# Second parts of 28 weight units kept in DRAM between two token groups of a diffusion layer kernel

## The chip, the cores and the metric

One core of one Trainium2 chip. The metric is the device time of one launch in microseconds. Three runs were made before the change; the figure is their median, and one more execution was profiled.

## The reference

A layer is run for 128 context tokens and for 1024 latent tokens with the same weights. What matters here, per group of tokens (shapes are tokens by features, D = 1024):

```python
h = rmsnorm(x, norm1_g) * (1.0 + scale1) + shift1
z = h @ w_in                      # zu, zv, zq, zf_fw, zf_bw, zi, zg, za, zb
y_a = chunk_gmlp(zu, zv, ...)     # gated mixing inside chunks of 128 tokens
y_b, s_fin = hgrn2_bidir(zq, zf_fw, zf_bw, zi, zg, ...)      # two scans over all tokens
mix = (sigmoid(za) * (y_a @ w_proj_a) + sigmoid(zb) * (y_b @ w_proj_b)) @ w_out
x = x + gate1 * mix
h = rmsnorm(x, norm2_g) * (1.0 + scale2) + shift2
q = (h @ w_q).reshape(n_tok, 8, 2, 128)
s = einsum('thpc,hpkc->thpk', q, sub_keys)    # 16 score rows of 128 keys for each token
# top 16 of each row, best 16 of the sums of two rows, softmax: 128 experts for each token
x = x + gate2 * sum_e gelu(h . u_tab[e]) * g_e * v_tab[e]
```

All inputs and outputs are float32.

## The kernel before

The tokens are nine tiles of 128: tile 0 is the context, tiles 5 to 8 are group GA, tiles 1 to 4 group GB. The kernel goes through these stages: modulation vectors (`ada`), the context's scan and its group, the scans of all eight latent tiles (4 heads), `group(GA)`, `group(GB)`, and the dense expert stage.

The weights come in units of 128 x 1024 values, stacked in `wst` in the order of their use. `unit(u)` (line 181) loads a unit through SP's DMA queue into one of three buffers `wraw`. A float32 product is made of three fast ones (`mmx`, line 124): each operand is a rounded part H and the rest L, and H times H, L times H and H times L are added up. So for the latent tokens `unit` makes two tiles of each unit with `split` (line 98): ScalarE copies the raw values into `wH` with rounding, and VectorE subtracts `wH` from the raw values into `wL`. `wH` and `wL` have two buffers each. The context's group uses the raw values as they are (`native`).

One call of `group` (line 571) runs over these units, counted from `U_GR` = 16: 0 to 3 and 4 to 7 give rows of zg and zv for the four tiles of the group (`proj_rows`, 24 matmuls of 512 columns for a unit), 8 to 11 give zu, then 24 units give za, zb and the two mixing projections in turn, 8 give w_out, and 44 to 59 are the sixteen query units. For each query unit TensorE makes the queries (`pq`) and then the scores against 128 keys for each of the four tiles (`psc`), and VectorE takes the top 16 of each tile with `top16` (line 414): five passes over 128 values with three loads of match values.

Work of a group that was done before fills in. `combine` (choosing the best 16 of 256 sums, on VectorE) and `build_G` (matrices of gate values for the dense experts, on TensorE, ScalarE and VectorE) wait in lists, and `tick()` at each unit puts a few steps of them into the program. Tokens of tiles 0 to 3 take their experts by `gather` (line 801): for each of 256 rows POOL issues an indirect load of one expert row for each of 128 tokens into one of four buffers, and VectorE multiplies it (`jk`, line 814) or adds it up (`acc`, line 829). Such VectorE instructions are `paced`: a scheduler may not put them ahead of the instruction that is `anchors[0]`, the subtraction of some units ago.

The instructions of each engine are put in order by a scheduler that works by its own costs; on the chip each engine and each DMA queue runs its list in order. POOL's queue takes the gathers, the few small POOL instructions, two loads of 2 MB (`hTBr`) and two of 2.5 MB (`h2DH`, `h2DL`, line 990) from DRAM. All else is on SP's queue.

Of the kernel before, what the change touches and what calls it, by code (L numbers as in the profile page):

```python
# [9 lines left out]
F32 = mybir.dt.float32  # L10
# [5 lines left out]
AF = mybir.ActivationFunctionType  # L16
# [23 lines left out]
GI = 4  # L40

U_ZI, U_HG, U_GR = 0, 4, 16
GATHER = [0, 1, 2, 3]
DENSE = [5, 6, 7, 8, 4]
ND = len(DENSE)
# [6 lines left out]
def hybrid_kernel(ctx, tc, x_all, pos, c2t, w_ada, b_ada, wst, wspt, bsp, lbraw, vecs, fng, skt, state,  # L52
                  ut, urow, vrow, masks, ident_d, small, y_p, y_s, ns):
    nc = tc.nc
    V, A, P, G = nc.vector, nc.scalar, nc.tensor, nc.gpsimd

    consts = ctx.enter_context(tc.tile_pool(name="consts", bufs=1, side="left", reuse_waits="tile"))
    dram = ctx.enter_context(tc.tile_pool(name="dram", bufs=1, space=bass.MemoryType.DRAM))
# [14 lines left out]
    o_d = dram.tile([NT, 128, 512], F32, name="o_d")  # L73
    tvi_d = dram.tile([NT, 128, 512], F32, name="tvi_d")
    h2r_d = dram.tile([NT, 128, D], F32, name="h2r_d")


    ident = consts.tile([128, 128], F32, name="ident")
# [18 lines left out]

    def split(src, H, L):
        A.activation(H, src, AF.Copy)  # L99
        return V.tensor_tensor(out=L, in0=src, in1=H.bitcast(F32), op=OP.subtract)  # L100

    anchors = deque()

    def anchor(ins, keep):

        anchors.append(ins)
        while len(anchors) > keep:
            anchors.popleft()
# [34 lines left out]
    wp = ph1.enter_context(tc.tile_pool(name="wp", bufs=2, side="right", reuse_waits="tile"))  # L143

    nload = [0]

    def load_unit(src, native=True):

# [32 lines left out]
    def unit(u, native=False, src=None):  # L181
        tick()
        raw = load_unit(wst[u] if src is None else src, native)
        if native:
            return [raw]
        H = wp.tile([128, 1024], F32R, name="wH", bufs=2)
        L = wp.tile([128, 1024], F32R, name="wL", bufs=2)
        anchor(split(raw, H, L), 2)
        return [H, L]


# [220 lines left out]
    GA, GB = [5, 6, 7, 8], [1, 2, 3, 4]  # L412

    def top16(gp, s, v_, i_, n, V=V):
        V.max(v_[:, 0:8], s)
        V.max_index(i_[:, 0:8], v_[:, 0:8], s)
        m = s if gp is None else gp.tile([128, 128], F32, name="mrep", bufs=2)
        V.match_replace(m[:, :n], v_[:, 0:8], s, -3.0e38)
        V.max(v_[:, 8:16], m[:, :n])
        V.max_index(i_[:, 8:16], v_[:, 8:16], m[:, :n])  # L420

    def combine(gp, t, tv, ti, al=None, c4=None, V=V, h0=0, h1=8, res=None):

# [147 lines left out]
    def group(gp, tiles, hpar, native):  # L571
        n = len(tiles)
# [37 lines left out]
        u = U_GR  # L610
# [126 lines left out]
        tv = [gp.tile([128, 8, 2, 16], F32, name="tv", bufs=n) for _ in range(n)]  # L737
# [6 lines left out]
        for b in range(16):  # L744
            if b == 8:
                for i in split_at:
                    res = gp.tile([128, 384], F32, name="res", bufs=1).rearrange("p (a b) -> p a b", a=3)
                    halves[i] = res
                    choose_q.append(combine(gp, tiles[i], tv[i], ti[i], h1=4, res=res))
                    rate["choose"] = 1.5  # L750
            w = unit(u + 44 + b, native)
            skb = gp.tile([128, 128], F32, name="skb", bufs=2)
            nc.sync.dma_start(skb, skt[:, b, :])
            ps = pmm("pq")
            projT(ps[:, :T], w, opd_q)
            qs = h512("qs")
            A.activation(qs[:, :T], ps[:, :T], AF.Copy)
            pss = ptp("psc")
            for i in range(n):
                P.matmul(pss[:, i * 128:(i + 1) * 128], qs[:, i * 128:(i + 1) * 128], skb, start=True, stop=True)  # L760
            for i in range(n):
                top16(gp, pss[:, i * 128:(i + 1) * 128], tv[i][:, b // 2, b % 2, :], ti[i][:, b // 2, b % 2, :], 128)
        rate["gather"] = before
        for i in range(n):
            t = tiles[i]
# [217 lines left out]
    for z in range(2):  # L983
        G.dma_start(hTBr[z], hT_d[z])
    rate.update(gather=RATE[2], choose=RATE[3], build=RATE[5])
    group(gp, GB, hTBr, False)
    rate.update(choose=0, gather=0, build=0)
    h2D = bigpair("h2D", TD)
# [214 lines left out]
```

## Time and profile before

| | |
|---|---|
| runs | 3636.42, 3621.89, 3634.37 us; median 3634.37 us |
| the profiled execution | 3629.96 us |
| its span, first to last instruction | 3628.2 us |
| TensorE matmuls busy | 3336.8 us (92% of the span) |
| VectorE busy | 2817.6 us (78%) |
| ScalarE, POOL busy | 1121.3 us (31%), 1429.2 us (39%) |
| moved from and to DRAM | 971.12 MB, mean 268 GB/s |

Read the busy shares as means over stages: the dense stage, from 1727 us to the end, is more than half of the span. PE in the tables is TensorE's matmul, PEld its weight load, DVE is VectorE, ACT ScalarE, SP the engine whose queue issues most transfers. The matmuls of one stage overlap in the profile, so the distance from one start to the next tells more than one duration.

### The profile page before, as it was taken

How to read it: one execution, taken by the hardware profiler on the slowest of the kernel's cores; microseconds unless marked ns; L12 is line 12 of the kernel's file. 1: busy time of each engine (PE TensorE's matmuls, PEld its weight loads, DVE VectorE, ACT ScalarE, POOL GpSimd, SP SyncE). 2: the span in 40 equal slices, each digit the busy share in tenths (PEclk: the TensorE clock that was granted, in tenths of full speed). 3: DMA queues.
4: the chain of work that ended last, by engine and by line, in shares of the span. 5: the costliest groups of instructions: out<-in, count | busy, mean ns of one | idle time of the engine just before them, and what ended most of it. 6: DMA issues, size and time to landing. Idle time of an engine off the chain costs nothing. (4 is left out here: it accounts for less than half of the span.)

```text
span 3628.2 us, 48825 instructions
## 1 busy us (share of the span) xinstructions
PE 3336.8 (92%) x17547; PEld 2764.3 (76%) x17547; DVE 2817.6 (78%) x5427; ACT 1121.3 (31%) x2095; POOL 1429.2 (39%) x1128
## 2 busy tenths in 40 slices
PE   8898999899887999877889999989999999999997
PEld 4386888775665676666788898889898888898996
DVE  2317678785899888697888888888887888788887
ACT  2512443321323655625322222222222222222222
POOL 0102102553112322200365664655555456555653
PEclk9899999999999999999999999999999999999998
DMA  7787324789534778643898997998998799988986
GB/s 282 287 294 274 113 72 132 257 313 342 168 127 141 271 255 325 248 144 117 291 332 299 326 327 268 336 326 306 324 319 320 245 343 333 324 305 316 337 320 247
DMA packets 361957, 971.12 MB, mean 268 GB/s; under 512 B 32721, under 2 KB 142673, under 8 KB 356081
## 3 DMA queue, kind: packets, MB, share of 16 engines
q0 software_dynamic: 149824, 546.37, 42.4%
q1 hardware_dynamic: 211888, 421.62, 33.6%
q8 instruction: 138, 2.26, 0.3%
q14 instruction: 107, 0.87, 0.1%
HBM read 897.07 MB, written 70.80 MB: 267 GB/s over the span
## 5 line engine op out<-in xcount | busy, mean ns | idle before, releaser
L811 POOL DMA_INDIRECT gu<-in_urow_dram,ix x512 | 688.2, 1344 | 1004.7 <-DVE jk L814 421.9
L824 POOL DMA_INDIRECT gv<-in_vrow_dram,ix x512 | 687.3, 1342 | 819.5 <-DVE acc L829 412.2
L814 DVE SCALAR_TENSOR_TENSOR jk<-gu,h2r 128x1024 f16<-128x1024 f32 x512 | 625.2, 1221 | 127.9 <-DMA gu<-in_urow_dram,ix 121.8
L829 DVE SCALAR_TENSOR_TENSOR acc<-gv,act,acc 128x1024 f32<-128x1024 f32 x508 | 651.3, 1282 | 45.2 <-DMA gv<-in_vrow_dram,ix 37.5
L129 PE MATMUL pH<-h2DH,uH 128*128 128x320 f32 x2016 | 626.5, 311 | 10.6 <-DVE accd L1061 8.2
L131 PE MATMUL pH<-h2DH,uL 128*128 128x320 f32 x2016 | 623.7, 309 | 1.1 <-DVE uL L100 1.1
L130 PE MATMUL pH<-h2DL,uH 128*128 128x320 f32 x2016 | 624.2, 310 | 0.0
L129 PEld LDWEIGHTS pH<-h2DH,uH 128*128 128x128 f32 x2016 | 380.4, 189 | 21.7 <-DVE accd L1061 13.4
L130 PEld LDWEIGHTS pH<-h2DL,uH 128*128 128x128 f32 x2016 | 380.4, 189 | 4.5
L131 PEld LDWEIGHTS pH<-h2DH,uL 128*128 128x128 f32 x2016 | 380.2, 189 | 1.7 <-DVE uL L100 1.7
L129 PE MATMUL pout<-vH,aH 128*128 128x512 f32 x768 | 300.6, 394 | 21.9 <-ACT vH L99 16.1
L99 ACT ACTIVATE vH<-vr 128x1024 fp32r<-128x1024 f32 x128 | 133.2, 1058 | 564.0 <-DMA vr<-in_vrow_dram 295.8
L131 PE MATMUL pout<-vH,aL 128*128 128x512 f32 x768 | 301.7, 393 | 4.1 <-DVE aL L100 4.1
L130 PE MATMUL pout<-vL,aH 128*128 128x512 f32 x768 | 301.7, 393 | 1.1 <-DVE vL L100 1.1
L129 PE MATMUL prot<-vH,aH 128*128 128x512 f32 x512 | 209.2, 409 | 54.4 <-DVE accd L1061 50.1
L99 ACT ACTIVATE wH<-wraw 128x1024 fp32r<-128x1024 f32 x118 | 124.9, 1058 | 401.9 <-PE pq L130 163.7
L100 DVE TENSOR_TENSOR vL<-vr,vH 128x1024 fp32r<-128x1024 f32 x128 | 156.1, 1220 | 91.0 <-ACT vH L99 90.9
L560 PE MATMUL pG<-oh 128*128 128x128 f16 x1280 | 176.8, 316 | 33.3 <-ACT Gs L563 21.6
L560 PEld LDWEIGHTS <-oh 128*128 128x128 f16 x1280 | 147.2, 131 | 78.0 <-issue 63.2
L130 PE MATMUL prot<-vL,aH 128*128 128x512 f32 x512 | 206.2, 403 | 0.0
L131 PE MATMUL prot<-vH,aL 128*128 128x512 f32 x512 | 205.5, 401 | 0.0
L99 ACT ACTIVATE aH<-a 128x640 fp32r<-128x640 f32 x128 | 94.2, 737 | 358.3 <-DVE a L1078 352.2
(345 smaller groups left out, 6306.4 us busy)
## 6 DMA issues: line engine op xcount, KB each, us to landing
wraw<-in_wst_dram SPq DMA_DIRECT2D x216, 512.0 KB, 4.6
vr<-in_vrow_dram SPq DMA_DIRECT2D x128, 512.0 KB, 6.8
ur<-in_ut_dram SPq DMA_DIRECT2D x126, 512.0 KB, 6.6
G_d<-Gs SPq DMA_DIRECT2D x40, 1024.0 KB, 5.0
Gt<-G_d SPq DMA_DIRECT2D x160, 256.0 KB, 9.6
wraw<-in_w_ada_dram SPq DMA_DIRECT2D x48, 512.0 KB, 5.5
gu<-in_urow_dram,ix POOLq DMA_INDIRECT x512, 6.7
gv<-in_vrow_dram,ix POOLq DMA_INDIRECT x512, 6.9
```

Source lines behind the costliest of these rows:

```text
L99: A.activation(H, src, AF.Copy)
L100: return V.tensor_tensor(out=L, in0=src, in1=H.bitcast(F32), op=OP.subtract)
L129: P.matmul(ps, a[0], b[0], start=first, stop=False)
L130: P.matmul(ps, a[0], b[1], start=False, stop=False)
L131: P.matmul(ps, a[1], b[0], start=False, stop=last)
L560: P.matmul(pg[:, :, tt], oh[:, 0, :, tt], og[a][:, :, tt], start=(a == 0), stop=(a == 1))
L811: G.indirect_dma_start(out=ur, out_offset=None, in_=urow, in_offset=bass.IndirectOffsetOnAxis(ap=ix[:, c:c + 1], axis=0))
L814: paced(V.scalar_tensor_tensor(jk, ur, 1.0, h2r, op0=OP.mult, op1=OP.mult, accum_out=dots[:, k:k + 1]))
L824: G.indirect_dma_start(out=vr, out_offset=None, in_=vrow, in_offset=bass.IndirectOffsetOnAxis(ap=ix[:, c:c + 1], axis=0))
L829: paced(V.scalar_tensor_tensor(acc, vr, act[:, k:k + 1], acc, op0=OP.mult, op1=OP.add))
```

## The change

For 28 of the 60 units of a group, 0 to 11 and 44 to 59 (`KEPT`), the first latent group GA writes `wL` to DRAM on SP's queue after the subtraction. The second group GB loads and rounds the raw unit as before, but takes `wL` from DRAM by a load on POOL's queue in place of the subtraction. For these units there is no anchor in GB any more; in the queries the last instruction of the first tile's `top16` becomes one.

```diff
+KEPT = set(range(0, 12)) | set(range(44, 60))
...
+    wL_d = dram.tile([60, 128, 1024], F32, name="wL_d")
...
+    second = [False]
...
         H = wp.tile([128, 1024], F32R, name="wH", bufs=2)
         L = wp.tile([128, 1024], F32R, name="wL", bufs=2)
+        if src is None and u - U_GR in KEPT and second[0]:
+            A.activation(H, raw, AF.Copy)
+            G.dma_start(L, wL_d[u - U_GR])
+            return [H, L]
         anchor(split(raw, H, L), 2)
+        if src is None and u - U_GR in KEPT:
+            nc.sync.dma_start(wL_d[u - U_GR], L.bitcast(F32))
         return [H, L]
...
-        V.max_index(i_[:, 8:16], v_[:, 8:16], m[:, :n])
+        return V.max_index(i_[:, 8:16], v_[:, 8:16], m[:, :n])
...
             for i in range(n):
-                top16(gp, pss[:, i * 128:(i + 1) * 128], tv[i][:, b // 2, b % 2, :], ti[i][:, b // 2, b % 2, :], 128)
+                ins = top16(gp, pss[:, i * 128:(i + 1) * 128], tv[i][:, b // 2, b % 2, :], ti[i][:, b // 2, b % 2, :], 128)
+                if i == 0 and tiles is GB:
+                    anchor(ins, 2)
...
     rate.update(gather=RATE[2], choose=RATE[3], build=RATE[5])
+    second[0] = True
     group(gp, GB, hTBr, False)
```

The scheduler orders the program anew. Line numbers in the changed program are a few higher: 193 is the new load of L, 197 its store, 157 the load of the raw weights, 762 that of the keys (`skb`), 822 and 835 the gathers, 1002 the loads for the dense stage.

POOL at the start of GB, before. The rows are gathers of expert rows (`gu`, `gv`) and the small instructions of a norm:

```order
L824 DMA gv<-in_vrow_dram,ix_2105 128x1024 x9
L811 DMA gu<-in_urow_dram,ix_2105 128x1024 x5
L94 TENSOR_SCALAR rstd<-ss 128x1
L95 TENSOR_TENSOR rstd<-rstd,nhalf 128x1
L94 TENSOR_SCALAR rstd<-ss 128x1
```

The same place with the change:

```order
L835 DMA gv<-in_vrow_dram,ix_2106 128x1024 x9
L822 DMA gu<-in_urow_dram,ix_2106 128x1024
L193 DMA wL<-wL_d 128x1024
L822 DMA gu<-in_urow_dram,ix_2106 128x1024
L193 DMA wL<-wL_d 128x1024
L822 DMA gu<-in_urow_dram,ix_2106 128x1024
L193 DMA wL<-wL_d 128x1024 x2
L822 DMA gu<-in_urow_dram,ix_2106 128x1024
L193 DMA wL<-wL_d 128x1024
L822 DMA gu<-in_urow_dram,ix_2106 128x1024
L193 DMA wL<-wL_d 128x1024 x4
L822 DMA gu<-in_urow_dram,ix_2106 128x1024 x3
```

The loads for the first nine units of GB stand between the gathers, four of them in a row; three more follow among the norm's instructions.

SP at the first queries of GA, before. `h2T_d` takes the normed tokens for the dense stage, `wraw` is a unit's load:

```order
L734 DMA h2T_d<-h2L 128x4x128 x2
L753 DMA skb<-in_skt_dram 128x128
L154 DMA wraw<-in_wst_dram 128x1024
L753 DMA skb<-in_skt_dram 128x128 x2
L154 DMA wraw<-in_wst_dram 128x1024 x2
```

With the change:

```order
L743 DMA h2T_d<-h2L 128x4x128 x2
L197 DMA wL_d<-wL 128x1024
L762 DMA skb<-in_skt_dram 128x128 x2
L157 DMA wraw<-in_wst_dram 128x1024
L762 DMA skb<-in_skt_dram 128x128
L197 DMA wL_d<-wL 128x1024
L157 DMA wraw<-in_wst_dram 128x1024
L197 DMA wL_d<-wL 128x1024
L157 DMA wraw<-in_wst_dram 128x1024
```

A store of L now stands ahead of each load of raw weights.

POOL at the queries of GB, before:

```order
L95 TENSOR_TENSOR rstd<-rstd,nhalf 128x1 x2
L990 DMA h2DH<-h2T_d 128x5120
L990 DMA h2DL<-h2T_d 128x5120
L824 DMA gv<-in_vrow_dram,ix_2105 128x1024 x3
L94 TENSOR_SCALAR rstd<-ss 128x1
```

With the change:

```order
L193 DMA wL<-wL_d 128x1024 x2
L1002 DMA h2DH<-h2T_d 128x5120
L193 DMA wL<-wL_d 128x1024
L835 DMA gv<-in_vrow_dram,ix_2106 128x1024
L193 DMA wL<-wL_d 128x1024
L835 DMA gv<-in_vrow_dram,ix_2106 128x1024
L1002 DMA h2DL<-h2T_d 128x5120
L193 DMA wL<-wL_d 128x1024 x2
L835 DMA gv<-in_vrow_dram,ix_2106 128x1024 x2
L193 DMA wL<-wL_d 128x1024
L835 DMA gv<-in_vrow_dram,ix_2106 128x1024
L193 DMA wL<-wL_d 128x1024 x7
```

The loads of L for the third query on stand around the two loads for the dense stage and around the last gathers of the first gathered tile.

## Rows read from the trace of the kernel before

**Rows 1.** The page's first line.

```profile
span 3628.2 us, 48825 instructions
```

**Rows 2.** Busy time by stretch of the span; the columns stand in the first row.

```profile
core 0: us, PE busy (x) PEld busy (x) DVE busy (x) ACT busy (x) POOL busy (x), PEclk, DMA share, GB/s
600.00:700.00 100.00, 86.16 (x437) 70.44 (x436) 77.92 (x125) 36.97 (x70) 48.11 (x38) 0.91 0.64 210
925.00:1036.00 111.00, 107.32 (x516) 85.91 (x515) 102.22 (x493) 30.24 (x42) 13.34 (x10) 0.98 0.51 162
1036.00:1138.00 102.00, 83.37 (x355) 65.20 (x354) 97.60 (x408) 36.70 (x53) 14.47 (x16) 0.92 0.34 108
1138.00:1200.00 62.00, 51.46 (x224) 36.33 (x223) 57.99 (x177) 24.57 (x56) 15.02 (x12) 0.94 0.47 161
1200.00:1500.00 300.00, 274.24 (x1418) 193.30 (x1417) 255.79 (x442) 169.25 (x498) 101.85 (x81) 0.97 0.80 293
1530.00:1653.00 123.00, 101.63 (x473) 80.98 (x472) 111.84 (x574) 27.85 (x37) 6.73 (x7) 0.92 0.42 146
1727.00:3628.00 1901.00, 1799.25 (x9888) 1624.31 (x9888) 1588.90 (x2146) 471.77 (x689) 1056.10 (x784) 0.97 0.89 312
```

**Rows 3.** TensorE's waits from 1036 to 1140 us: total us, times, longest.

```profile
PE prow L130 <- DVE wL L100: 9.9, 2, 5.9
PE pzu L131 <- DVE wL L100: 6.3, 1, 6.3
```

**Rows 4.** TensorE's groups, 1524 to 1665 us: count | busy, mean ns | idle before.

```profile
L131 PE MATMUL pq<-h2H,wL 128*128 128x512 f32 x123 | 50.6, 415 | 16.8 <-DVE wL L100 16.8
```

**Rows 5.** VectorE's groups, 1036 to 1140 us.

```profile
L100 DVE TENSOR_TENSOR wL<-wraw,wH 128x1024 fp32r<-128x1024 f32 x12 | 14.6, 1215 | 1.5 <-ACT wH L99 1.5
```

**Rows 6.** VectorE's groups, 1524 to 1665 us.

```profile
L100 DVE TENSOR_TENSOR wL<-wraw,wH 128x1024 fp32r<-128x1024 f32 x16 | 19.3, 1213 | 9.5 <-ACT wH L99 9.5
```

**Rows 7.** Score matmuls in GA and GB (ns, first and last start), and TensorE's timeline.

```profile
L760 PE MATMUL psc<-skb,qs x128: 272/275/315, 937.3 to 1039.6; 128*128 128x128 f32 x128
...
L760 PE MATMUL psc<-skb,qs x128: 275/275/377, 1529.3 to 1652.6; 128*128 128x128 f32 x128
...
1609.36 1.09 PE L760 MATMUL psc<-skb,qs 128*128 128x128 f32 x8
...
1621.98 1.07 PE L760 MATMUL psc<-skb,qs 128*128 128x128 f32 x8
...
1646.62 0.40 PE L129 MATMUL pq<-h2H,wH 128*128 128x512 f32 x1
...
1649.66 0.39 PE L130 MATMUL pq<-h2L,wH 128*128 128x512 f32 x1
```

**Rows 8.** Timeline of VectorE (first two) and SP's queue: start us, us.

```profile
957.24 1.21 DVE L100 TENSOR_TENSOR wL<-wraw,wH 128x1024 fp32r<-128x1024 f32 x1
963.84 1.22 DVE L100 TENSOR_TENSOR wL<-wraw,wH 128x1024 fp32r<-128x1024 f32 x1
...
958.48 0.33 SPq L154 DMA_DIRECT2D wraw<-in_wst_dram  x1
965.08 0.58 SPq L154 DMA_DIRECT2D wraw<-in_wst_dram  x1
```

**Rows 9.** Timeline of POOL: start us, us, in brackets idle before and its end.

```profile
957.32 1.95 POOL L824 DMA_INDIRECT gv<-in_vrow_dram,ix  x1 [16.82 <-DVE ti L420]
960.11 0.94 POOL L824 DMA_INDIRECT gv<-in_vrow_dram,ix  x1 [0.85 <-DVE acc L829]
...
1088.28 1.86 POOL L811 DMA_INDIRECT gu<-in_urow_dram,ix  x1 [26.18 <-DVE cp L420]
```

**Rows 10.** DMA issues: count, KB each, median us from issue to landing.

```profile
wraw<-in_wst_dram SPq DMA_DIRECT2D x216, 512.0 KB, 4.6
...
gu<-in_urow_dram,ix POOLq DMA_INDIRECT x512, 6.7
...
x_d<-xr SPq DMA_DIRECT2D x9, 512.0 KB, 3.3
...
h2DH<-h2T_d POOLq DMA_DIRECT2D x1, 2560.0 KB, 10.0
```

## The prediction

> **What bounds the kernel now.** I read the page's first part, the table of busy time by stage, then who waits for whom in the stages that the change touches. The span is 3628.2 us [rows 1]; the profiled execution took 3629.96 us, 1.8 us more, and stands 4.4 us under the median of the three runs, 3634.37 us. My sum is made against 3629.96 us. About 0.5% (18 us) is what a measurement here can tell from no change.
>
> In the table by stage [rows 2] the reader is to see three kinds of stage. From 1727 us on comes the dense expert stage, 1901 us: TensorE is busy 1799 us of it, and nothing there is edited. From 1200 to 1500 us TensorE is busy 274 of 300 us. But in the two ends of the second group VectorE is the full engine: 97.6 of 102 us while its twelve first units are projected (1036 to 1138 us), 58.0 of 62 us just after, and 111.8 of 123 us in its queries (1530 to 1653 us). There TensorE waits for VectorE, and for exactly the instruction that the change removes: 9.9 and 6.3 us for the subtraction that makes L in the first stage [rows 3], 16.8 us in the queries [rows 4]. The first group's queries (925 to 1036 us) show the same full VectorE, 102.2 of 111 us [rows 2].
>
> **The change part by part, against 3629.96 us.**
>
> *Removed.* 28 subtractions in the second group. Twelve take 14.6 us in the first stage, 1215 ns each [rows 5]; sixteen take 19.3 us in the queries, 1213 ns each [rows 6]. The rounding on ScalarE that makes H stays, and so does the load of the raw weights.
>
> A, first stage: does the whole 14.6 us count? TensorE's own work there is twelve units of 24 matmuls. Fourteen matmuls in a row of 512 columns start from 1646.62 to 1649.66 us [rows 7], 0.234 us apart, so a unit is 5.6 us and twelve are 67 us, well under the 87 us that 102 - 14.6 leaves. VectorE stays the bound: **-14.6 us**. The stage after it is full on VectorE too, and the one after that is a loop of TensorE, ScalarE and VectorE in which nothing changes, so the time is kept.
>
> B, queries: VectorE's 111.8 us fall to 92.5. TensorE's floor comes from two sets of score matmuls that start two units apart, at 1609.36 and 1621.98 us [rows 7]: 6.31 us a unit, 95 us for the fifteen units between first and last set, which now take 123.3 us (1529.3 to 1652.6 us [rows 7]). Both floors lie under 123 - 19.3 = 104 us, so the gain lies between 19.3 us (VectorE's idle time stays as it is) and 28 us (TensorE at its floor). I take **-19.3 us**: the first group did 16 units with their subtractions in 102.3 us [rows 7], so 104 with the choosing added has precedent.
>
> *Added in the second group.* 28 loads of L, 512 KB each, on POOL's queue among the gathers. No row shows such a load from POOL in this place. A buffer of L comes free when TensorE ends the unit two before; a load then costs about 0.94 us on POOL, as a gather does [rows 9], and 4.6 us to land, as the raw weights take from SP's queue [rows 10]: 5.5 us, against the 5.6 us of the unit that covers it. So the cover is just enough, without reserve.
>
> C: from 0 (each is just in time) to 1 us a unit, 12 us (POOL comes late, since a gather before it waits for VectorE to free a row: POOL idled 26.18 us before one gather in this stage [rows 9]). In the order of the change VectorE frees the rows for the gathers ahead of each of these loads before the place at which it used to subtract for that unit. So I take the lower part: **+3 us**.
>
> The Trainium skill speaks against putting these loads on POOL: SBUF — State Buffer, section "SBUF: two separate sides", says that GpSimd writes the descriptors of its own DMAs and is locked out while VectorE holds the port pair that they share. The trace has something like it: a gather that starts in VectorE's full stretch took 1.95 us, the next one 0.94 us [rows 9]. By the row alone I charge 0.94 us; what the rule would make of the sum is a rival below.
>
> D: two loads of 2560 KB for the dense stage stand in the same queue, ahead of the loads for the fifth and the seventh query; the first took 10.0 us to land [rows 10]. An L load behind one has a unit's time, 6.3 us, as cover: 3.7 us late at most, twice, so 0 to 7 us; **+3 us**, as VectorE has top-16 work of a unit in reserve there.
>
> By DMA: Bandwidth & Descriptors of the Trainium skill, section "Anatomy of one DMA", 512 KB from POOL would take 2.0 us and 1.2 us more for the bytes, 3.2 us (an estimate by that page's figures). The nearest row says 4.6 us for SP's loads of that size [rows 10]; by the page's figure C would be near its lower end, by the row it is without reserve.
>
> *Added in the first group.* 28 stores of L on SP's queue. Each waits for its subtraction, and SP does nothing else meanwhile. What stands behind it is the load three units on, and that one waits for the same instruction already: the subtractions at 957.24 and 963.84 us end at 958.45 and 965.06 us, and the loads start at 958.48 and 965.08 us [rows 8]. So the store adds only its own issue, 0.33 us [rows 8]. Its transfer (3.3 us for a store of this size [rows 10]) falls in stages where the DMA engines are busy 0.64 and 0.51 of the time [rows 2]. E: 0 to 28 x 0.33 = 9 us; as three raw buffers give a lead of two units, **+1 us**.
>
> *Moved.* In the second group only the first top-16 of a query paces the filling gathers, so a few gathers move earlier on VectorE within the first stage; their number is the same. F: the subtractions for the first two expert units used to be made between the last top-16s; now they follow them, so TensorE's work for these units starts later, by the top-16 work of the last query. That is bounded by 0 and by one unit of 6.3 us; **+2 us**, because VectorE's chain of choosing, not TensorE, ends that stretch.
>
> Sum: -14.6 - 19.3 + 3 + 3 + 1 + 2 = -24.9 us, so **3605 us**. The dense stage keeps its 1901 us and begins earlier.
>
> **The rivals.**
>
> *POOL paces the second group.* The full 12 of C and 7 of D come due: -33.9 + 12 + 7 + 1 + 2 = -12 us, 3618 us. For it: POOL's long waits on VectorE [rows 9] and a cover without reserve. Against it: in the order, VectorE frees the rows of the gathers ahead of each load earlier than it made L before. Chance 0.17.
>
> *Loads held while VectorE reads two operands.* If each of the twelve first loads is held as the longer gather was, 1.95 - 0.94 = 1.0 us [rows 9], the cover of 5.5 becomes 6.5 us against 5.6, and 12 x 0.9 = 11 us go: 3605 + 11 = 3616 us. The rows bear it out half: the short gather stands in the same stretch. Chance 0.07. This is what the lock on that page of the Trainium skill, SBUF — State Buffer, would do here.
>
> *The first stage's gain is absorbed* by the loop from 1200 to 1500 us: 14.6 and most of C drop out, 3605 + 12 = 3617 us. Against it: TensorE is not idle there for want of time but in a fixed order. Chance 0.05.
>
> *Slower: gathers behind L loads.* POOL is in order, so a gather behind a load waits until TensorE has ended a unit, and VectorE, in order too, waits at that gather's multiplication with the choosing behind it. The place is the run of four loads in a row with three gathers after it, in the first stage, where 11 gathers in all stand behind loads. A gather takes 6.7 us to land [rows 10]. If six of the eleven come late by that, 40 us are added: 3645 us. It decides when VectorE reaches such a multiplication before the gather has landed. If TensorE is not held, its seventh unit ends at 1036 + 7 x 5.6 = 1075 us, and a gather behind the loads that wait for it lands some 8 us later, at 1083 us; before the change a gather in the middle of this stage was only issued at 1088.28 us [rows 9]. So it takes 5 to 10 us of lost time on TensorE first. Chance 0.11.
>
> That the change does nothing is excluded by the order: 28 loads, 28 stores, 28 subtractions fewer. The forecast keeps 0.60.
>
> **How the numbers follow.** Within the forecast the bounds give 3587 us (B at 28, C to F at nothing) to 3626 us (C, D and E at their upper ends). A range of 3588 to 3630 us takes in the three cases near 3617 us and leaves out the slow one and about 0.08 of tails. More than 0.5% faster means under 3612 us: nearly all of the forecast and a little of the cases at 3616 to 3618 us, 0.63. Within 0.5%: the rest of those and the forecast's bad end, 0.26. Slower: 0.11.
>
> **What would show it.** Right: VectorE loses 28 subtractions; TensorE's waits for L in the first stage and in the queries nearly vanish; first to last score set of the second group takes 100 to 107 us instead of 123; the first twelve units end about 10 us sooner; the first group keeps its times within 2 us. Wrong: TensorE waits for the DMA of L by more than 10 us in all; VectorE waits for gathers in the first stage; the first group's loads land later and its stages stretch; or the dense stage starts earlier but lasts longer.

## The result and the profile after

The change makes the kernel faster: 3614.24 us, the median of 20 runs (3596.41 to 3628.27), against 3632.94 us before (3621.89 to 3640.61, 20 runs). The ratio is 0.9949, with a 95% interval from 0.9939 to 0.9959: 18.7 us less, where 24.9 us less had been forecast. The profiled execution is the fastest of the 20, 18 us under their median; so a second profile of the change, and one of the kernel before, stand among the experiments.

The page's first lines:

```profile
span 3594.3 us, 48910 instructions
...
PE 3326.4 (93%) x17547; PEld 2757.1 (77%) x17547; DVE 2786.3 (78%) x5399; ACT 1125.0 (31%) x2097; POOL 1447.2 (40%) x1156
```

The busy time by stage, with the columns and stages of [rows 2]; only the last stage ends elsewhere, with the span:

```profile
925.00:1036.00 111.00, 105.26 (x505) 84.35 (x506) 99.23 (x476) 33.63 (x47) 14.08 (x12) 0.97 0.67 219
1036.00:1138.00 102.00, 94.35 (x411) 73.69 (x410) 94.40 (x428) 41.59 (x59) 27.24 (x31) 0.95 0.63 216
1138.00:1200.00 62.00, 52.45 (x228) 34.93 (x227) 58.02 (x173) 25.99 (x64) 14.08 (x11) 1.00 0.51 172
1200.00:1500.00 300.00, 263.40 (x1374) 185.94 (x1373) 242.31 (x427) 168.10 (x493) 95.88 (x81) 0.96 0.77 282
1530.00:1653.00 123.00, 111.75 (x555) 91.87 (x555) 115.53 (x657) 32.72 (x45) 15.29 (x22) 0.96 0.62 219
1727.00:3594.00 1867.00, 1778.94 (x9833) 1608.94 (x9831) 1572.73 (x2059) 465.45 (x680) 1062.98 (x784) 0.98 0.90 315
```

The window from 1036 to 1138 us holds other work now than before, as the stages moved. So here is the stage by its own marks, from the last score set of the first group to the first block sum `pzab` of the second, before (first row) and with the change:

```profile
1039.60:1138.40 98.80, 80.17 (x339) 62.60 (x339) 94.40 (x391) 35.22 (x52) 14.80 (x16) 0.91 0.34 108
1046.20:1128.70 82.50, 77.07 (x339) 60.65 (x338) 77.40 (x369) 35.92 (x53) 23.89 (x27) 0.95 0.62 206
```

The stage is 16.3 us shorter, and VectorE has 17.0 us less to do in it. The twelve subtractions are 14.6 us of these [rows 5]; the rest is filling work that the new order puts elsewhere, so it is no gain of the kernel. TensorE's waits from 1036 to 1140 us (first two rows), and in the queries from 1528 to 1630 us (last row), are:

```profile
PE prow L132 <- DMA wL<-wL_d: 2.8, 2, 1.8
...
PE pvs L645 <- ACT gv L638: 1.9, 1, 1.9
...
PE pq L133 <- DMA wL<-wL_d: 2.2, 2, 1.8
```

The waits of 9.9 and 6.3 us and the idle 16.8 us [rows 3, 4] for L's subtraction are gone; 2.8 and 2.2 us for the DMA of L stand in their place. The score matmuls of the first and of the second group (duration in ns, first and last start), to be held against [rows 7]:

```profile
L769 PE MATMUL psc<-skb,qs x128: 270/275/417, 941.2 to 1046.2; 128*128 128x128 f32 x128
...
L769 PE MATMUL psc<-skb,qs x128: 270/275/377, 1528.0 to 1629.4; 128*128 128x128 f32 x128
```

First to last score set of the second group takes 101.4 us instead of 123.3. But the first set starts only 1.3 us earlier than before, though the first units (the column of that name below) took some 13 us less: much was lost on the way there. To see where, I cut each profiled execution at six marks. The columns are: the start to the first group's first score set (GA); from there to the second group's first block sum `pzab` (first units); the block sums; from the last of them to the second group's first score set (w_out and norm); from there to the end of VectorE's last top-16 (queries); to the first matmul of the dense stage's own units (choosing); and the rest (dense). All in us.

| execution | GA | first units | block sums | w_out, norm | queries | choosing | dense |
|---|---|---|---|---|---|---|---|
| before | 937.3 | 201.1 | 256.0 | 134.9 | 128.9 | 73.9 | 1896.1 |
| before, second profile (b1_before) | 930.5 | 200.2 | 256.1 | 134.8 | 128.6 | 74.0 | 1900.0 |
| the change | 941.2 | 187.5 | 258.7 | 140.6 | 112.0 | 74.5 | 1879.8 |
| the change, second profile (a1_again) | 944.2 | 188.4 | 261.2 | 141.6 | 112.4 | 74.4 | 1892.8 |
| e1_first12 | 944.8 | 187.8 | 262.0 | 134.4 | 128.0 | 74.6 | 1907.0 |
| e2_queries | 933.3 | 202.7 | 260.2 | 136.1 | 111.6 | 76.0 | 1898.7 |
| e3_stores | 944.4 | 202.5 | 259.8 | 135.7 | 128.6 | 73.9 | 1902.9 |
| g1_one_store | 938.8 | 202.4 | 260.0 | 134.9 | 127.2 | 74.6 | 1888.1 |
| e4_no_transfer | 934.1 | 184.0 | 256.6 | 136.8 | 108.1 | 74.6 | 1895.3 |
| e10_loads_only | 931.8 | 187.4 | 261.0 | 142.7 | 111.8 | 74.3 | 1893.4 |
| e5_tail | 939.7 | 187.1 | 260.8 | 136.6 | 112.3 | 74.7 | 1891.0 |
| e6_sp_queue | 945.1 | 184.1 | 260.6 | 140.3 | 122.0 | 75.8 | 1902.3 |
| f2_without_44_45 | 940.0 | 190.3 | 261.5 | 135.6 | 112.6 | 76.2 | 1898.4 |
| f1_first_on_sp | 947.1 | 184.9 | 258.9 | 137.2 | 110.9 | 74.8 | 1890.6 |

Three columns are sharp: first units, queries and choosing repeat within 1 us in the two profiles of the kernel before and in the two of the change (kernels that make the first units alike spread a little more, 200.2 to 202.7 us). Three are blunt. The dense stage takes 1880 to 1907 us in kernels whose dense stage is the same, block sums 256.0 to 262.0, and the start 930 to 947. So single executions settle the sharp columns, and only ratios of many runs settle a total.

### The profile page after: what moved, and what is told of

It is laid out like the page before. It is cut to its first block, busy times and chain, and to the rows that moved or that the text cites. A ratio compares the mean times of both kernels' runs of the same rounds, so it can differ in the third digit from the quotient of the medians.

```text
span 3594.3 us, 48910 instructions
## 1 busy us (share of the span) xinstructions
PE 3326.4 (93%) x17547; PEld 2757.1 (77%) x17547; DVE 2786.3 (78%) x5399; ACT 1125.0 (31%) x2097; POOL 1447.2 (40%) x1156
## 5 line engine op out<-in xcount | busy, mean ns | idle before, releaser
L101 ACT ACTIVATE uH<-ur 128x1024 fp32r<-128x1024 f32 x126 | 133.4, 1058 | 240.4 <-PE pH L132 221.4
## 6 DMA issues: line engine op xcount, KB each, us to landing
Gt<-G_d SPq DMA_DIRECT2D x160, 256.0 KB
```

## The experiments

**Each half of the change alone.**

```diff
e1_first12
-KEPT = set(range(0, 12)) | set(range(44, 60))
+KEPT = set(range(0, 12))
...
-                if i == 0 and tiles is GB:
+                if False:
e2_queries
-KEPT = set(range(0, 12)) | set(range(44, 60))
+KEPT = set(range(44, 60))
```

> Only the twelve first units of a group (0 to 11) go through DRAM; the queries of the second group subtract and anchor as before. My theory: the first stage of the second group gets shorter by about 14 us, as in the profile of the change (99.2 to 85.4 us from the last score set of the first group to the first block sum of the second), but some 6 us of it are lost before the first score set of the second group (there the change was only 1.3 us ahead), and the tail, whose order is as before, loses nothing. So 6 to 12 us less than before, ratio 0.9967 to 0.9983. Rival 1, the first-stage gain is wholly absorbed by the loop that follows: ratio 0.999 to 1.001. Rival 2, all of it is kept: 14 us, ratio 0.996.

Measured: ratio 0.9987 [0.9973, 1.0002], 1.2 us between the medians and at most 10. The first units took 187.8 us, 13 us less than before, as expected, and w_out, norm and queries kept their times. The total misses what was expected: 0.9987 lies between the theory (0.9967 to 0.9983) and rival 1 (0.999 to 1.001), and the interval holds parts of both; rival 2's 0.996 is outside. Most of what the first units gained is not seen in the runs. The start and the block sums of this execution are among the longer ones of the table.

> Only the sixteen query units (44 to 59) go through DRAM; the first twelve units subtract as before. My theory: first to last score set of the second group takes about 101 us instead of 123 us, 22 us less, and about 5 us are given back because the subtractions of the first two expert units come behind the last top-16; with a microsecond or two for the stores 14 to 17 us less, ratio 0.9953 to 0.9962. Rival 1, the whole gain of the change comes from the queries: 18 to 19 us, ratio 0.9949, and the kernel with the first twelve alone shows nothing. Rival 2, POOL's loads profit from the earlier stage having drained the gathers, so that alone the queries gain less than 12 us, ratio over 0.9967.

Measured: ratio 0.9974 [0.996, 0.9988], 9.4 us less by it. First to last score set took 100.9 us and the queries to VectorE's last top-16 111.6 us, 17 us less than before; so rival 2's reason (POOL's loads gain only behind a drained queue) falls by the marks. The total misses what was expected (0.9953 to 0.9962) and has the value that rival 2 named (over 0.9967); why less of it shows in the runs than in the marks is open. Rival 1 falls with it: the queries alone do not give the 18.7 us. Neither half accounts for the whole.

**The stores alone, and one store.**

```diff
e3_stores
-        if src is None and u - U_GR in KEPT and second[0]:
+        if src is None and u - U_GR in KEPT and False:
...
-        if src is None and u - U_GR in KEPT:
+        if src is None and u - U_GR in KEPT and not second[0]:
...
-                if i == 0 and tiles is GB:
+                if False:
g1_one_store, on top of this
-KEPT = set(range(0, 12)) | set(range(44, 60))
+KEPT = {59}
```

> The first group writes its 28 L parts to DRAM, and the second group subtracts and anchors as before; nobody reads the stored parts. Every engine but SP has the same list of instructions as before the change. My theory: the stores stretch the first group's queries from 102.3 to about 105 us, and little else: 1 to 4 us more, ratio 1.0003 to 1.0011. Rival 1, SP's stores that wait for a subtraction delay the loads of raw weights behind them in all three stages: 9 us, ratio 1.0025, and waits of VectorE and ScalarE for raw weights in the first group. Rival 2, the store costs nothing and the 2.7 us in the profile of the change are drift of one execution: ratio 0.9997 to 1.0003.

Measured: ratio 1.0004 [0.9989, 1.002], so between 4 us less and 7 us more; rival 1's 9 us are outside. The first group's queries did not stretch, as the row of the score sets shows; VectorE's waits there come behind it:

```profile
L769 PE MATMUL psc<-skb,qs x128: 272/275/347, 944.4 to 1047.0; 128*128 128x128 f32 x128
```

```profile
DVE wL L102 <- ACT wH L101: 2.6, 1, 2.6
DVE tv L424 <- PE psc L769: 1.6, 4, 0.6
```

First to last start is 102.6 us, where before it was 102.3 [rows 7] and with the change 105.0, and VectorE waits 4.2 us in the whole stretch, for H and scores and no raw weights. So my theory on that place falls: the 2.7 us are no cost of the stores alone. In the change TensorE waits 1.8 us, at 1043 us, for the first L load of the second group while the first group's last scores are still to be made. POOL issued it at 1035.38 us, when the buffer came free, and the next one only at 1041.43 us, with a gather between:

```profile
1035.38 0.59 POOL L193 DMA_DIRECT2D wL<-wL_d  x1 [1.93 <-PE pq L133]
1037.79 0.99 POOL L822 DMA_INDIRECT gu<-in_urow_dram,ix  x1 [1.82 <-DMA wraw<-in_wst_dram]
1041.43 0.57 POOL L193 DMA_DIRECT2D wL<-wL_d  x1 [2.66 <-PE pq L133]
```

The load alone does not make it either. In e1_first12, which stores nothing in the queries, and in e10_loads_only, which stores nothing at all, the same load from POOL brings no wait of TensorE, and first to last start is 102.3 us in both. It takes both: stores in the first group's queries and the load on POOL's queue (104.4 us in the second profile of the change, 104.8 in e5_tail, 105.8 in f2_without_44_45). With the load on SP's queue it is 102.7 us (e6_sp_queue) and 102.2 us (f1_first_on_sp). Why the load lands late there is not shown.

The stores are not free by the profiles, though: in the eight executions of kernels that store the first twelve L parts the column GA reads 939.7 to 947.1 us, in the six others 930.5 to 938.8 (a division made after the numbers were seen). A part of that, 3 us on average, is there when the first scan's projections begin (364.1 against 360.7 us), well before the first store is issued (568.8 us in the change); in e3_stores all engines have the lists of before until then. That led to the last run:

> The kernel before with the DRAM space for 60 L parts and one store only, that of the last query unit of the first group (at about 1030 us); the second group subtracts as before. In four profiled executions of kernels without a store the first scan's projections (ph) begin at 358.8 to 359.9 us, in nine with stores at 360.2 to 369.1 us, 5 us later on average, though the first store is issued at 568 us and no engine has another list of instructions until then. My theory: the space in DRAM, by which all other scratch tensors lie elsewhere, makes the loads of this stage slower, and not the stores; then ph begins at 361 us or later here, and the ratio to before is 1.0005 to 1.002. Rival: it is the 28 stores (by what they add to the program, or by chance of these executions); then ph begins below 360 us and the ratio is 0.999 to 1.0005.

Measured: ratio 1.0001 [0.9987, 1.0015], and the first scan's projections begin at 359.2 us. So the space in DRAM alone costs nothing that 12 runs can show (at most some 5 us), and the rival holds. What makes the start of the kernels with many stores longer stays open; by the ratio of e3_stores it is at most 7 us.

**Without transfers, and with loads alone.**

```diff
e4_no_transfer
-            G.dma_start(L, wL_d[u - U_GR])
-            return [H, L]
+            return [H, H]
...
-        if src is None and u - U_GR in KEPT:
-            nc.sync.dma_start(wL_d[u - U_GR], L.bitcast(F32))
e10_loads_only
-            G.dma_start(L, wL_d[u - U_GR])
+            G.dma_start(L, wst[u])
...
-        if src is None and u - U_GR in KEPT:
-            nc.sync.dma_start(wL_d[u - U_GR], L.bitcast(F32))
```

> The second group makes no L part for the 28 units and uses H in its place (so the product of L and the tokens is replaced by one of H and the tokens, with the same number of matmuls); no store in the first group and no load in the second. This is the change with its transfers at no price. My theory: the loads are hidden but for a few microseconds and the stores cost about 3 us, so 20 to 25 us less than before, ratio 0.9931 to 0.9945, and first to last score set of the second group again about 100 us, since TensorE is the bound there by then. Rival 1, waiting for the loads of L costs 6 us and more in the first stage and the queries: 28 us or more less than before, ratio under 0.9925. Rival 2, the transfers cost nothing: ratio 0.9949 as with the change.

This kernel leaves L out and puts H in its place, e10_loads_only puts other weights there; neither computes the layer, and only their times are used. Measured: ratio 0.9907 [0.9888, 0.9927], 33.6 us less between the medians. My theory falls here, and rival 1 holds, at the edge of the interval: the transfers cost about 15 us (33.6 - 18.7). Even so the queries took 108.1 us to VectorE's last top-16, 20.6 us less than before, and first to last score set 97.0 us, near the floor of 95 us that B was worked out with.

> The second group loads a unit of raw weights, rounded, in the place of L (so the product of L and the tokens is one of the wrong values, with the same number of matmuls), from POOL's queue with the same bytes as in the change; the first group stores nothing. The kernel without any transfer was 33.6 us faster than before, the change 18.7 us, so loads and stores together would cost some 15 us. My theory: the loads cost it, 4 us in the queries, 3 us at the first units, and the stores next to nothing (stores alone 1.0004): ratio as the change, 0.9940 to 0.9955. Rival: the stores cost it where the group's other stages are full (GA), then ratio 0.991 to 0.993.

Measured: ratio 0.9939 [0.9926, 0.9952], within what was expected. Between the two kernels lie 0.0032 of 3632 us, 11.6 us, for the loads alone (the two intervals just touch, so the size is rough). By the table they are: 3.4 us in the first units (187.4 against 184.0), 3.7 in the queries (111.8 against 108.1), and 5.9 in w_out and norm (142.7 against 136.8), where the next but one experiment shows how much single executions differ. The page's DMA part says how long such a load takes:

```profile
wL<-in_wst_dram POOLq DMA_DIRECT2D x28, 512.0 KB, 4.3
```

4.3 us to land, near SP's 4.6 us [rows 10].

**The change again.** The same kernel.

> The changed kernel itself once more, for a second profile. The profiled execution of the change lay 18 us under the median of its own 20 runs, and its dense stage (first to last matmul of the hidden layer) took 1840 us against 1854 us before. My theory: that is chance of one execution; here the dense stage takes 1850 to 1865 us, the profile of the second group keeps its marks (first stage about 83 to 86 us, queries 101 us, tail 85 us), and the ratio to before is again 0.9940 to 0.9965. Rival: the change shortens the dense stage itself; then it takes 1838 to 1845 us again.

Measured: 0.9949 [0.9935, 0.9962], and the hidden layer of the dense stage took 1852.9 us. The gain in the dense stage of the first profile was chance of one execution.

**Where some of the expected gain may have gone: w_out.** In the change, POOL's timeline in w_out (start us, us, in brackets idle before and what ended it) reads:

```profile
1433.57 0.59 POOL L193 DMA_DIRECT2D wL<-wL_d  x1
...
1449.16 0.94 POOL L835 DMA_INDIRECT gv<-in_vrow_dram,ix  x1 [0.30 <-issue]
1461.60 0.56 POOL L193 DMA_DIRECT2D wL<-wL_d  x1 [11.49 <-PE prow L129]
1462.47 1.35 POOL L835 DMA_INDIRECT gv<-in_vrow_dram,ix  x1 [0.30 <-issue]
```

These are the loads for the first two queries. The scheduler put them far ahead, among the gathers; the second one's buffer was still read by a matmul of w_out, since `load_unit` uses buffers of `wL` for raw w_out units too. POOL stood 11.49 us there, with gathers behind. VectorE's waits in the change from 1387 to 1484 us (a total, times, longest) now hold a row for gathered `gv` rows, 3.4 us, and TensorE's wait for VectorE's `oh` (the row behind) is 3.9 us, where it was 1.2 us before:

```profile
DVE jk L825 <- DMA gu<-in_urow_dram,ix: 8.1, 4, 4.5
DVE oh L541 <- PE pG L569: 6.2, 9, 1.9
DVE acc L840 <- DMA gv<-in_vrow_dram,ix: 3.4, 1, 3.4
```

```profile
PE pG L569 <- DVE oh L549: 3.9, 3, 2.0
```

The row of before (1393 to 1490 us):

```profile
PE pG L560 <- DVE oh L540: 1.2, 1, 1.2
```

The kernel without these two loads:

```diff
f2_without_44_45
-KEPT = set(range(0, 12)) | set(range(44, 60))
+KEPT = set(range(0, 12)) | set(range(46, 60))
```

> The change without units 44 and 45, the first two queries, which the second group subtracts as before. In the profile of the change POOL stands 11.5 us (1449 to 1461 us) at the load of L for one of them, whose buffer a matmul of w_out still reads, with gathers behind it; VectorE then waits 3.4 us for a gathered row and TensorE 3.9 us for VectorE. My theory: this load, in order in POOL's queue, is what makes the stretch from the last block sum (pzab) to the last w_out row 95.9 and 96.9 us long against 90.8 before; here it takes 91 to 93 us, VectorE waits for no gathered gv row there, and as VectorE is not full while the tokens are normed the two subtractions cost nothing: 3 to 5 us less than the change, ratio 0.9930 to 0.9945. Rival: the scheduler's other order of the filling work makes the 5 us; the stretch stays at 95 to 97 us and the ratio at 0.9949.

Its waits of VectorE in the same stretch:

```profile
DVE jk L825 <- DMA gu<-in_urow_dram,ix: 7.2, 4, 4.7
DVE oh L541 <- PE pG L569: 4.7, 6, 1.6
DVE oh L541 <- ACT oh L545: 0.5, 1, 0.5
```

The wait for `gv` is gone. The last matmuls of w_out start, in the second profile of before, in the change and here (`prow`, last start):

```profile
L127 PE MATMUL prow<-wraw,mg x128: 590/592/626, 1392.4 to 1480.6; 128*128 128x512 f32 x128
```

```profile
L129 PE MATMUL prow<-wraw,mg x128: 590/592/1128, 1389.5 to 1484.6; 128*128 128x512 f32 x128
```

```profile
L129 PE MATMUL prow<-wraw,mg x128: 590/592/626, 1393.8 to 1484.7; 128*128 128x512 f32 x128
```

Counted from the last block sum (1386.8, 1387.4 and 1391.8 us) that is 93.8, 97.2 and 92.9 us. (The expectation counted to the first matmul of the last group; by that mark it is 90.8, 95.9 and 90.8.) In its place that is what the theory expected, 135.6 us for w_out and norm instead of 140.6 and 141.6. The total did not follow: ratio 0.995 [0.9935, 0.9965], the change's, and the rival's number. The first units (190.3 us) and the stretch of choosing (76.2) took 2 us more each in this execution; 5 us lie inside the interval.

Other runs do not let this load stand as the cause. Two rows of e6_sp_queue, which has no load of L on POOL (1389.8 to 1530.1 us):

```profile
DVE acc L840 <- DMA gv<-in_vrow_dram,ix: 3.0, 2, 2.9
PE pG L569 <- DVE oh L549: 5.5, 5, 2.0
```

The waits that were put down to the load are there without it, and w_out and norm take 140.3 us. And e5_tail (the next experiment), in which the four engines run the same order as the change in this stretch, has the load's wait in full, yet takes 136.6 us:

```profile
1460.30 0.56 POOL L194 DMA_DIRECT2D wL<-wL_d  x1 [11.49 <-PE prow L129]
```

What differs between these two is TensorE's granted clock. From the last block sum to the first score set, the change (first row) and e5_tail:

```profile
1387.40:1528.00 140.60, 119.28 (x577) 78.89 (x575) 91.94 (x171) 82.94 (x222) 32.87 (x38) 0.92 0.71 260
1387.60:1524.20 136.60, 115.13 (x577) 75.12 (x575) 92.00 (x171) 82.49 (x222) 32.87 (x38) 0.95 0.72 266
```

The same 577 matmul records are busy 4.15 us less, which is the 4.0 us between the two stretches; TensorE's longest row of waits is 12.7 us in both. So 4 of the 6 us are what two executions of one order can differ by, and f2_without_44_45, which also has another order of filling work, separates nothing. The 11.49 us of POOL are shown; that they cost the kernel time is not, and why w_out and norm took longer in both profiles of the change stays open.

**The end of the queries.**

```diff
e5_tail, at the last query of GB
             A.activation(qs[:, :T], ps[:, :T], AF.Copy)
+            if tiles is GB and b == 15:
+                for e in range(2):
+                    pre.append(unit(0, src=ut[e]))
...
-        u = unit(0, src=ut[e])
+        u = pre[e]
```

> The change, with the two first expert units loaded and split inside the last query of the second group, ahead of its top-16, in place of behind it; only VectorE's order differs, in that the two subtractions stand ahead of the last four top-16 instead of at their end. My theory: the tail from the last score set to the dense stage goes back from 85 to 86 us to about 80 us, 5 us less, and the queries stay at 101 us: ratio to before 0.9925 to 0.9950, and 5 us less than the change in the same session. Rival: the tail is set by the chain of choosing on VectorE, which the order of two subtractions does not shorten; tail 85 us, ratio as the change.

Measured: ratio 0.9947 [0.9933, 0.9961]; from the last score set to the dense stage 85.9 us. The rival holds: putting the two subtractions ahead does not shorten it. The timelines of VectorE show where it ends. Before (first row; it ends the last row of top-16) and with the change (second row):

```profile
1657.92 0.28 DVE L420 FIND_INDEX8 ti<-tv,mrep 128x8 uint32<-128x128 f32 x1
```

```profile
1639.70 0.28 DVE L429 FIND_INDEX8 ti<-tv,mrep 128x8 uint32<-128x128 f32 x1
```

Before, VectorE ended 5.6 us after the last score set (1658.2 against 1652.6 us); with the change 10.6 us after it (1640.0 against 1629.4). TensorE ran ahead, VectorE followed, and from VectorE's last top-16 to the dense stage all kernels take 73.9 to 76.2 us (column choosing).

**The loads on the other queue.**

```diff
e6_sp_queue
-            G.dma_start(L, wL_d[u - U_GR])
+            nc.sync.dma_start(L.bitcast(F32), wL_d[u - U_GR])
f1_first_on_sp, with KEPT of f2_without_44_45
-            G.dma_start(L, wL_d[u - U_GR])
+            if u - U_GR < 12:
+                nc.sync.dma_start(L.bitcast(F32), wL_d[u - U_GR])
+            else:
+                G.dma_start(L, wL_d[u - U_GR])
```

> The change, with the 28 loads of L issued on SP's queue among the loads of raw weights instead of on POOL's. My theory: in the queries the loads of L stand on POOL behind the two loads of 2560 KB and land late, which costs some 4 us there, and 2 to 3 us at the first units; on SP's queue they are 3 to 5 us faster where POOL was late, but each holds the raw loads behind it until its buffer of L is free, so that H may be late: between 4 us less and 6 us more than the change, ratio 0.993 to 0.997. First to last score set 97 to 101 us if POOL was the cause. Rival: the buffers and not the queue set the time, 101 us and the same ratio as the change.

Measured: ratio 0.9948 [0.9929, 0.9966], as expected, by two effects against each other. The first units took 184.1 us, as without any transfer (184.0): on SP's queue these loads cost nothing that the mark shows. The queries took 122.0 us, 10 us more than with the change, and first to last score set 111.4 us, where 97 to 101 had been expected; so both the theory and the rival fail there. The 6 us more that the two marks leave are not seen in the total, whose interval is 7 us to either side. TensorE's waits there, and those of SP's queue:

```profile
PE pq L133 <- DMA wL<-wL_d: 8.6, 2, 5.0
```

```profile
SPq L193 <- PE pq L133: 35.6, 12, 4.0
SPq L762 <- PE psc L769: 30.4, 13, 8.4
```

SP's queue stood 30.4 us before loads of the keys, up to 8.4 at a time, until score matmuls freed a buffer, and 35.6 us before the L loads themselves, with raw weights and keys behind them. POOL's queue is the better one in the queries, SP's in the first units; f1 takes both.

> As the kernel without units 44 and 45, and the twelve loads of the first units on SP's queue, those of the queries on POOL's. My theory: with all loads on SP's queue the first group's queries took 102.7 us instead of 104.4 to 105.0 us (there the load for the first unit of the second group came late on POOL), and the first stage 81.4 us instead of 82.5 and 84.0; so another 2 to 4 us less, ratio 0.9920 to 0.9940, with the queries at 101 us. Rival: SP's loads of L wait for their buffers and hold the raw loads behind them, here as in the queries where that cost 10 us: ratio 0.995 or more, first stage 85 us or more.

Measured: 3602.35 us, ratio 0.992 [0.9904, 0.9936], 29 us less than before by it and clearly under the change's 0.9949. The total gained more than the 2 to 4 us that were expected: f2_without_44_45, from which this kernel differs by the queue of the twelve loads, stands at 0.995, 11 us more. First units 184.9 us against 190.3 there, the first group's queries 102.2 us (947.1 to 1049.3), queries 110.9 against 112.6; the remaining 4 us are not placed. The waits of TensorE in the first units hold no row for L's DMA any more:

```profile
PE pzab L133 <- DVE wL L102: 2.3, 1, 2.3
PE pyb L627 <- DVE th L619: 2.0, 2, 1.2
PE pzu L131 <- ACT wH L192: 1.6, 1, 1.6
```

It is the fastest version here that computes the reference.

**The kernel before again.**

> The kernel before, once more, for a second profile. My theory: the marks of its stages that do not depend on the order of chance repeat within 1 us: first stage of the second group 98 to 100 us, last block sum to last w_out row 90.5 to 92 us, queries 122.5 to 123.5 us, last top-16 5.6 us after the last score set; the stage of block sums and gating, where single executions of all kernels lay between 256.0 and 262.0 us, and the time at which the first scan ends (577.6 to 586.6 us) vary. Rival: the loop takes 256 us again and the scan ends at 580 us again, so that the change's 259 to 261 us and 585 to 587 us are its own cost.

Measured: the sharp marks repeated within 1 us (200.2, 93.8 us for block sum to w_out, 123.0 us for the score sets). The block sums took 256.1 us again, as the rival says. But g1_one_store and e3_stores, whose second group has the same lists on TensorE, VectorE and POOL as before, took 260.0 and 259.8; so the change's 258.7 and 261.2 are not shown to be its own.

## Why the prediction was right, and what it missed

The direction and the mechanism were right: the subtraction of L was what TensorE waited for. The size was right within 6 us, 18.7 us less against the 24.9 forecast; the median of 3614.24 us is 9 us above 3605 because the kernel before, too, measured 3 us above the base of the sum. That the total came this near is in part luck, as the last terms below show. Step by step:

- **A with C (-14.6 + 3 = -11.6):** the first units took 187.5 and 188.4 us against 201.1 and 200.2, -12.7. Without transfers it is -16.7 (184.0), so C is 4 us, forecast 3. A alone came out 2 us over its 14.6, about the filling work that left the stage. Its floor for TensorE, 67 us, was low, as it counts the projections alone: TensorE is busy 77.07 us of the stage's 82.5 with the change, VectorE 77.40, so VectorE is the bound by little. C lies partly where I had not looked, in the last queries of the first group, where the first unit's load is late; these took 2.1 to 2.7 us longer, over the 2 us that the prediction allowed.
- **B with D and F (-19.3 + 3 + 2 = -14.3):** queries and choosing together took 186.5 and 186.8 us against 202.8 and 202.6, -16. Without transfers 182.7, so the loads cost 4 us there (forecast 3 for D), and B with F is -20. The longest single wait for L in the queries was 1.8 us, under the 3.7 us of the bound.
- **F** was wrong as a mechanism. The order of the two subtractions costs nothing (e5_tail). The +5 us that a look at TensorE alone would put there are VectorE's lag. "VectorE's chain of choosing, not TensorE, ends that stretch" was the right half of the sentence. The sum was hardly hurt: B without it came out 0.7 us over its 19.3.
- **E (+1, at most 9):** open. The runs of e3_stores say -4 to +7 us, the profiles 9 us on average, of which 3 arise where no store was issued yet.
- **What the sum left out** is the rest of the second group. A says of the loop behind the first stage that "nothing changes, so the time is kept". Behind that loop the order does change: two of the sixteen loads of B stand on POOL's queue as early as w_out, and w_out and norm took 140.6 and 141.6 us instead of 134.9 and 134.8. How much of these 6 us is the change's is open: 4 us of them an execution of the same order did not have. POOL's wait with gathers behind it is what the rival "gathers behind L loads" describes, in another place than the run of four loads for which I had priced it (there VectorE waited for no gather) and with no cost shown.
- **The remainder.** The two groups of terms above gained 3 us more than forecast, and w_out and norm lost 6; so the start, the block sums and the dense stage together must hold some 4 us more, of which the forecast had 1 (E). Between the profiles of before and of the change they differ by 4 to 12 us each, and in both directions, so single executions cannot place these 4 us. That 6 us were missing in the total and 6 us were lost in w_out and norm is no agreement.

The rival "the first stage's gain is absorbed" is not borne out for the loop that it names: without transfers the first units took 184.0 us and the block sums behind them 256.6, as before (256.0 and 256.1). That e1_first12 shows at most 10 of its 13 us in the runs leaves it open whether some other stage takes a part.

The rival "POOL paces the second group" (3618 us) came near in its total, but not by its price: C and D were 4 and 4 us, not 12 and 7. "Loads held while VectorE reads two operands" did not occur. The 28 loads on POOL took 0.53 to 0.63 us each, in VectorE's full stretch as elsewhere, less than the 0.94 us that I charged:

```profile
L193 POOL DMA_DIRECT2D wL<-wL_d x28: 527/552/629, 1035.4 to 1614.3; - x28
```

Nor did the loads land later from POOL's queue than from SP's, in the second profile of the change (first row) and in e6_sp_queue:

```profile
wL<-wL_d POOLq DMA_DIRECT2D x28, 512.0 KB, 4.4
wL<-wL_d SPq DMA_DIRECT2D x28, 512.0 KB, 4.4
```

The lock that the Trainium skill describes in SBUF — State Buffer, section "SBUF: two separate sides", is therefore not to be seen in these loads. That section names it for VectorE's two-port modes, and for two inputs in SBUF only against a GpSimd instruction that reads SBUF, so the rival was wider than the page; whether VectorE ran such an instruction beside these loads, no run here shows. The estimate by the Trainium skill, DMA: Bandwidth & Descriptors, section "Anatomy of one DMA", 3.2 us for 512 KB, is not borne out here: 4.4 us was measured, and the cover was as thin as the row of SP's loads had said.

## What to carry to other kernels

Moving the product of a busy engine through DRAM pays when that engine ends the stage; take the gain from its own busy time, and mark the stage's end where that engine ends, not where the engine it feeds does. A load that waits for a buffer is a wait for all that stands behind it in its queue: look in the order for the first loads of a series, which a scheduler may put stages ahead of their use, and for buffers that other tiles share. One change can want two queues: on SP's queue the load cost nothing that the marks show in the first stage, and 10 us in the queries. And before a longer stage of one profile gets a cause, look for another execution of the same order and compare the granted clock: here 4 us came and went that way.

## What the runs showed of the hardware

POOL's plain 512 KB loads were cheaper to issue (0.53 to 0.63 us) than the gathers of [rows 9] (0.94 to 1.95 us). TensorE's granted clock in the second group's queries was 0.92 before [rows 2], with waits of 16.8 us for L [rows 4]; without these waits it was 1.00, its upper level of 2.4 GHz:

```profile
1528.00:1630.00 102.00, 97.39 (x475) 78.14 (x474) 94.65 (x540) 27.86 (x37) 15.29 (x22) 1.00 0.75 260
```

In w_out and norm the clock differed between two executions of the same order, 0.92 and 0.95, and with it the time, 140.6 and 136.6 us. And kernels whose first group stores spent up to 9 us more until the first scan's projections begin (369.1 against 359.9 us and less), before any store is issued; one store did not bring it about, and its cause was not found.
